# Attention scores as three 64-row passes per head instead of two stacked 128-row products

## The chip, the cores and the metric

The kernel runs on one core of a Trainium2 chip. The metric is the device time of one execution in microseconds (us). A core has TensorE (in the profile PE, its weight loads PEld), VectorE (DVE), ScalarE (ACT), GpSimd (POOL) and SyncE (SP), which here issues all DMA transfers. Matrix products read two operands from on-chip memory (a stationary one, which is loaded as weights, and a moving one, which is streamed past it) and write into a PSUM bank of 512 float32 columns on 128 partitions.

## The reference

The reference is an encoder trunk of two layers on 512 tokens with a model width of 1024. Each layer projects its input once and feeds three token mixers: neighbourhood attention (8 heads of 64), differential attention (4 heads, each with two maps of 64) and latent attention (8 heads of 96). Their outputs are gated, merged and projected, and a SwiGLU FFN follows. What the change touches are the scores of the first two mixers:

```python
# neighbourhood: each query of a 8 x 64 grid sees 8 x 16 keys of it
sc = jnp.einsum('bnqhd,banchd->bhnqac', qb, kb, preferred_element_type=jnp.float32) * scale
...
# differential: two maps per head, each a dense softmax attention over all 512 keys
a1 = blocked_attention(q1, k1, v, scale)
a2 = blocked_attention(q2, k2, v, scale)
o = a1 - lam.astype(a1.dtype) * a2
```

In both, the sum of a score runs over 64 numbers, and `scale` is 1/8.

## The kernel before

All products are made in `float32r`, a float32 format of reduced precision. To come near float32, every operand is split into a high part and a low part (`split`: ScalarE copies the source into the rounded high part, VectorE subtracts that from the source), and a product is a sum of partial products. Projections use three of them, hi x hi, lo x hi and hi x lo (`mm3`, L156 to L158), with 128 rows of the array, since their sums run over multiples of 128.

A score sums over 64 numbers only, which is half of the array's rows. The kernel before fills the other half by stacking. `stacks_q` (L299) makes one tile per head with the high part of q on the head's own 64 rows and the low part on the other 64. `stacks_k` (L311) makes two tiles per head: the high part of k on both halves, and the low part on both halves, the second of which is a copy by DMA (`copy`, L297). Two matmuls of 128 rows then give all four partial products: (q hi, q lo) x (k hi, k hi) and (q hi, q lo) x (k lo, k lo).

The scores stand in two places:

- `na_pair` works on two heads, whose projections share one 128-row tile, and on four blocks `b` of 128 queries with 256 keys each. A block takes one PSUM bank of the kind `sc`, with the two heads side by side. Each head gets two matmuls of 256 columns (L378, L379). VectorE then adds the bias table and finds the maximum (L383), and ScalarE makes the exponentials (L386).
- `df_head` works on one head and four tiles `t` of 128 queries with all 512 keys. Each of the two maps `j` takes one `sc` bank and gets two matmuls of 512 columns (L476, L477). VectorE finds the maximum (L478), and ScalarE makes the exponentials (L479).

There are two `sc` banks, which are used in turn. Around the scores stand the transposes of the weights of attention (L395, L486), their products with the values (L405, L491, L492) and projections of other parts of the layer: `fill` names by a table (`PLAN`) which gate projections (G) and merges (M) are written behind which head. Tiles for q, k, values and activations come from a ring of 38 slots (`R`), so that a slot's next use waits for its last reader.

The order in which each engine gets its instructions is not the order of the code. The tile framework schedules the program with a simulated timeline and places each instruction where it would be ready by that timeline; it can pull matmuls that are written next to each other apart. Each engine then works through its own list in order, and waits are semaphores between the lists.

Of the kernel before, what the change touches and what calls it, by code (L numbers as in the profile page):

```python
# [12 lines left out]
OP = mybir.AluOpType  # L13
# [63 lines left out]
def f32(ap):  # L77
    return ap.bitcast(F32)
# [3 lines left out]
def trunk(ctx, tc, x, ln_in, w_in, feat, bias, lamv, w_mla, w_mlr, w_mlv, w_branch, w_out,  # L82
# [213 lines left out]
    def copy(dst, src):  # L296
        nc.sync.dma_start(f32(dst), f32(src))  # L297

    def stacks_q(p, scale):  # L299

        res = []
        for h in range(2):
            own, oth = (slice(0, 64), slice(64, 128))[::1 if h == 0 else -1]
            t = R.get()
            A.activation(t[own], p[own], AF.Copy, scale=scale)
            V.scalar_tensor_tensor(t[oth], p[own], scale, f32(t[own]), op0=OP.mult, op1=OP.subtract)
            res.append(t)
        return res

    def stacks_k(p):  # L310

        res = []
        for h in range(2):
            own, oth = (slice(0, 64), slice(64, 128))[::1 if h == 0 else -1]
            th, tl = R.get(), R.get()
            A.activation(th[own], p[own], AF.Copy)
            A.activation(th[oth], p[own], AF.Copy)
            V.tensor_sub(tl[own], p[own], f32(th[own]))
            copy(tl[oth], tl[own])
            res.append((th, tl))  # L320
        return res

    def ptsplit(p):
        pp = dp.tile([128, 1024], F32R, tag="PP", name="PP", bufs=2)
# [30 lines left out]
    def na_pair(l, p, vals):  # L355
        src = lambda a, b: [w_in[l, a:b, C_NQ + p * 128:C_NQ + (p + 1) * 128],
                            w_in[l, a:b, C_NK + p * 128:C_NK + (p + 1) * 128]]
        ch = wload_ks(src, 256, (4, 4))
        pq, pk = bank("acc"), bank("acc")
        gemm_w(pq, ch, slice(0, 128), XT, slice(0, S), KD)  # L360
        qs = stacks_q(pq, 0.125)
        gemm_w(pk, ch, slice(128, 256), XT, slice(0, S), KD)
        ks = stacks_k(pk)
        bt = []
        for h in range(2):
            b = H.get()
            nc.sync.dma_start(b[:, :768], bias[l, :, 2 * p + h, :])
            bt.append(b)
        o = (R.get(), R.get())
        o32 = dp.tile([128, 512], F32, tag="o32", name="o32", bufs=1)  # L370
        al, sh = vals
        for b in range(4):
            k0 = (0, 8, 24, 32)[b]
            pat = (0, 1, 1, 2)[b]
            sc = bank("sc").rearrange("p (h k) -> p h k", h=2)
            for h in range(2):
                q = qs[h][:, b * 128:(b + 1) * 128]
                T.matmul(sc[:, h], q, ks[h][0][:, k0 * 8:k0 * 8 + 256], start=True, stop=False)  # L378
                T.matmul(sc[:, h], q, ks[h][1][:, k0 * 8:k0 * 8 + 256], start=False, stop=True)  # L379
            pr = ptile().rearrange("p (h k) -> p h k", h=2)  # L380
            nm, ls = stat(2), stat(2)
            for h in range(2):
                V.tensor_tensor_reduce(out=pr[:, h], in0=sc[:, h], in1=bt[h][:, pat * 256:(pat + 1) * 256],  # L383
                                       op0=OP.add, op1=OP.min, scale=-1.0, scalar=3.0e38,
                                       accum_out=nm[:, h:h + 1])
                A.activation(pr[:, h], pr[:, h], AF.Exp, bias=nm[:, h:h + 1], scale=-1.0,  # L386
                             accum_out=ls[:, h:h + 1])
            rl = stat(2)
            V.reciprocal(rl, ls)
            for h in range(2):  # L390
                V.tensor_scalar(pr[:, h], pr[:, h], rl[:, h:h + 1], None, op0=OP.mult)
            pt = bank("tr").rearrange("p (a h q) -> p a h q", a=2, h=2)
            for a in range(2):
                for h in range(2):
                    T.transpose(pt[:, a, h], pr[:, h, a * 128:(a + 1) * 128], ident)  # L395
            pp = dp.tile([128, 1024], F32R, tag="PP", name="PP", bufs=2)
            split(pp[:, 0:512], pp[:, 512:1024], pt.rearrange("p a h q -> p (a h q)"))
            pp = pp.rearrange("p (s a h q) -> p s a h q", s=2, a=2, h=2)
            po = bank("pv").rearrange("p (h s q) -> p h s q", h=2, s=2)
            for h in range(2):  # L400
                for a in range(2):
                    c0 = k0 + 16 * a
                    v = (al if c0 % 16 == 0 else sh)[c0 // 16][p // 2]
                    v = v[:, (2 * p + h) % 4 * 128:((2 * p + h) % 4 + 1) * 128]
                    T.matmul(po[:, h], v, pp[:, :, a, h], start=a == 0, stop=a == 1)  # L405
            for h in range(2):
                own, oth = (slice(0, 64), slice(64, 128))[::1 if h == 0 else -1]
                oc = o32[own, tsl(b)]
                A.activation(oc, po[oth, h, 0], AF.Copy)
                V.tensor_add(oc, po[own, h, 0], oc)  # L410
                V.tensor_add(oc, po[own, h, 1], oc)
        split(*o, o32)
        R.put(*qs, *ks[0], *ks[1])
        H.put(*bt)
        return o

# [29 lines left out]
    def df_proj(l, h):  # L446
        src = lambda a, b: [w_in[l, a:b, C_DQ + h * 128:C_DQ + (h + 1) * 128],
                            w_in[l, a:b, C_DK + h * 128:C_DK + (h + 1) * 128]]
        ch = wload_ks(src, 256, (4, 4))
        stg = H.get()  # L450
        sv = stg.rearrange("p (t c) -> p t c", t=NT)
        for t in range(NT):
            p = bank("acc")[:, :256]
            gemm_x(p, ch, slice(0, 256), XT, tsl(t), KD)
            A.activation(sv[:, t], p, AF.Copy)
        rope(stg.rearrange("p (t g d) -> p t g d", t=NT, g=4)[:, :, :, 0:16], cosd, sind, 4, 8)
        pq, pk = bank("tr"), bank("tr")
        for t in range(NT):
            T.transpose(pq[:, tsl(t)], sv[:, t, 0:128], ident)
        qs = stacks_q(pq, 0.125)  # L460
        for t in range(NT):
            T.transpose(pk[:, tsl(t)], sv[:, t, 128:256], ident)
        ks = stacks_k(pk)
        H.put(stg)
        return qs, ks

    def df_head(h, qk, vals, nlam, sg):
        qs, ks = qk
        ost = dp.tile([128, 512], F32, tag="o32", name="ost", bufs=1)
        ov = ost.rearrange("p (t d) -> p t d", t=NT)  # L470
        for t in range(NT):
            pr = [ptile(), ptile()]
            nm, ls = stat(2), stat(2)
            for j in range(2):
                sc = bank("sc")
                T.matmul(sc, qs[j][:, tsl(t)], ks[j][0], start=True, stop=False)  # L476
                T.matmul(sc, qs[j][:, tsl(t)], ks[j][1], start=False, stop=True)  # L477
                V.reduce_max(nm[:, j:j + 1], sc, axis=AX.X, negate=True)  # L478
                A.activation(pr[j], sc, AF.Exp, bias=nm[:, j:j + 1], accum_out=ls[:, j:j + 1])  # L479
            rl, cf = stat(2), stat()  # L480
            V.reciprocal(rl, ls)
            V.scalar_tensor_tensor(cf, ls[:, 0:1], rl[:, 1:2], nlam, op0=OP.mult, op1=OP.mult)
            V.scalar_tensor_tensor(pr[0], pr[1], cf, pr[0], op0=OP.mult, op1=OP.add)
            pt = bank("tr")
            for k in range(NT):
                T.transpose(pt[:, tsl(k)], pr[0][:, tsl(k)], ident)  # L486
            ch_, cl_ = ptsplit(pt)
            po = bank("pv")
            for k in range(NT):
                v = vals[k][:, (h % 2) * 256:(h % 2) * 256 + 256]  # L490
                T.matmul(po[:, 0:256], ch_[:, tsl(k)], v, start=k == 0, stop=False)  # L491
                T.matmul(po[:, 0:128], cl_[:, tsl(k)], v[:, 0:128], start=False, stop=k == NT - 1)  # L492
            tmp = sp.tile([128, 128], F32, tag="otmp", name="otmp", bufs=2)
            A.activation(tmp, po[:, 128:256], AF.Copy, scale=rl[:, 0:1])
            V.scalar_tensor_tensor(ov[:, t], po[:, 0:128], rl[:, 0:1], tmp, op0=OP.mult, op1=OP.add)
            ss = stat()
            A.activation(tmp, ov[:, t], AF.Square, scale=128 ** -0.5, accum_out=ss)
            rpow(ss, ss, RMS_EPS)
            V.tensor_scalar(ov[:, t], ov[:, t], ss, None, op0=OP.mult)
        R.put(*qs, *ks[0], *ks[1])  # L500
        pt = bank("tr")
        for t in range(NT):
            T.transpose(pt[:, tsl(t)], ov[:, t], ident)
        o = (R.get(), R.get())
        split(*o, pt, scale=sg)
        return o
# [583 lines left out]
```

## Time and profile before

| | |
|---|---|
| Median of three runs | 1861.91 us (1861.42 to 1862.11) |
| Profiled execution | 1861.61 us, of which the profile's span is 1859.6 us |
| TensorE matmuls | 11200, all with 128 rows |
| TensorE busy | 1814.6 us, 98% of the span |
| VectorE, ScalarE, GpSimd busy | 1331.0, 905.3, 88.2 us |
| Score matmuls, neighbourhood | 128 of 128x256 (L378, L379), 31.2 us busy |
| Score matmuls, differential | 128 of 128x512 (L476, L477), 51.3 us busy |

A row of the groups names the line, the engine, the operation, the tiles written and read, the shape, the count, then the busy time, the mean time of one in ns, the idle time of the engine ahead of it and what ended that idle time. Matmuls are pipelined and their ends are modelled, so the mean time of one is more than the distance from one start to the next; a timeline (start in us, length in us) shows the distances. A wait row names who waited for whom, the total in us, how often, and the longest.

### The profile page before, as it was taken

How to read it: one execution, taken by the hardware profiler on the slowest of the kernel's cores; microseconds unless marked ns; L12 is line 12 of the kernel's file. 1: busy time of each engine (PE TensorE's matmuls, PEld its weight loads, DVE VectorE, ACT ScalarE, POOL GpSimd, SP SyncE). 2: the span in 40 equal slices, each digit the busy share in tenths (PEclk: the TensorE clock that was granted, in tenths of full speed). 3: DMA queues.
4: the chain of work that ended last, by engine and by line, in shares of the span. 5: the costliest groups of instructions: out<-in, count | busy, mean ns of one | idle time of the engine just before them, and what ended most of it. 6: DMA issues, size and time to landing. Idle time of an engine off the chain costs nothing.

```text
span 1859.6 us, 28547 instructions
## 1 busy us (share of the span) xinstructions
PE 1814.6 (98%) x11200; PEld 1617.4 (87%) x11200; DVE 1331.0 (72%) x2228; ACT 905.3 (49%) x1620; POOL 88.2 (5%) x165
## 2 busy tenths in 40 slices
PE   6999999999999899999999999999999999999997
PEld 5988899988878899999789888999888789999996
DVE  6478887665568977777756888866655698677766
ACT  3467776555433433434326677755554244343431
POOL 4100000000001000000001000000000000000001
PEclk9999999999999999999999999999999999999999
DMA  7453332223251233333445432322233512333332
GB/s 250 119 166 88 88 101 74 79 81 85 90 193 58 69 104 101 102 103 102 148 124 156 124 97 87 90 65 86 74 97 109 174 57 90 105 95 110 92 101 79
DMA packets 167765, 195.86 MB, mean 105 GB/s; under 512 B 8528, under 2 KB 132688, under 8 KB 167632
## 3 DMA queue, kind: packets, MB, share of 16 engines
q1 hardware_dynamic: 167632, 194.05, 34.5%
q8 instruction: 88, 1.44, 0.3%
q14 instruction: 45, 0.37, 0.1%
HBM read 177.24 MB, written 9.44 MB: 100 GB/s over the span
## 4 chain that ended last, share of the span: by engine, by line
PE 89%; DVE 4%; DMA 3%; ACT 2%; issue 1%; POOL 1%; POOLq 0%; SPq 0%; DVEq 0%; ACTq 0%
PE acc L156 18%; PE acc L157 18%; PE acc L158 18%; PE sc L778 11%; PE pv L778 8%; PE tr L648 2%; DVE wlo L139 1%; PE pv L491 1%; DMA raw<-in_w_ffn_in_dram 1%; ACT whi L138 1%; PE pv L656 1%; PE pv L655 1%; PE sc L477 1%; PE sc L632 1%; PE sc L631 1%
## 5 line engine op out<-in xcount | busy, mean ns | idle before, releaser
L139 DVE TENSOR_TENSOR wlo<-raw,whi 128x1024 fp32r<-128x1024 f32 (+4 forms) x242 | 288.0, 1191 | 137.0 <-ACT whi L138 132.2
L138 ACT ACTIVATE whi<-raw 128x1024 fp32r<-128x1024 f32 (+4 forms) x242 | 250.0, 1034 | 267.4 <-DMA raw<-in_w_ffn_out_dram 50.9
L138 ACT ACTIVATE whi<-f 128x1024 fp32r<-128x1024 f32 x100 | 104.9, 1057 | 222.4 <-PE acc L158 127.3
L156 PE MATMUL acc<-xth,whi 128*128 128x512 f32 x512 | 203.9, 398 | 0.1
L158 PE MATMUL acc<-xth,wlo 128*128 128x512 f32 x512 | 202.8, 396 | 0.0
L157 PE MATMUL acc<-xtl,whi 128*128 128x512 f32 x512 | 202.6, 396 | 0.0
L156 PE MATMUL acc<-whi,r 128*128 128x512 f32 (+1 forms) x504 | 194.7, 392 | 4.6 <-DVE f L711 3.9
L157 PE MATMUL acc<-wlo,r 128*128 128x512 f32 (+1 forms) x504 | 197.3, 391 | 1.1 <-DVE wlo L139 1.1
L158 PE MATMUL acc<-whi,r 128*128 128x512 f32 (+1 forms) x504 | 197.0, 391 | 0.0
L778 PE MATMUL pv<-r,whi 128*128 128x256 f32 x960 | 175.8, 282 | 9.9 <-DVE P L844 4.8
L156 PE MATMUL acc<-whi,xth 128*128 128x256 f32 (+2 forms) x544 | 161.6, 299 | 2.1 <-ACT whi L138 2.1
L157 PE MATMUL acc<-wlo,xth 128*128 128x256 f32 (+2 forms) x544 | 162.1, 299 | 1.3 <-DVE wlo L139 1.3
L158 PE MATMUL acc<-whi,xtl 128*128 128x256 f32 (+2 forms) x544 | 162.1, 299 | 0.0
L778 PEld LDWEIGHTS pv<-r,whi 128*128 128x128 f32 x960 | 148.2, 189 | 13.4 <-DVE P L844 5.2
L139 DVE TENSOR_TENSOR wlo<-f,whi 128x1024 fp32r<-128x1024 f32 x100 | 121.6, 1221 | 26.0 <-ACT whi L138 25.8
L778 PE MATMUL pv<-r,wlo 128*128 128x256 f32 x480 | 134.7, 281 | 0.0
L778 PE MATMUL sc<-xth,whi 128*128 128x256 f32 x480 | 133.9, 280 | 0.7 <-ACT P L833 0.7
L778 PE MATMUL sc<-xtl,whi 128*128 128x256 f32 x480 | 133.7, 279 | 0.0
L778 PE MATMUL sc<-xth,wlo 128*128 128x256 f32 x480 | 133.3, 279 | 0.0
L156 PEld LDWEIGHTS acc<-whi,r 128*128 128x128 f32 x504 | 94.3, 188 | 26.9 <-DVE f L711 4.7
L157 PEld LDWEIGHTS acc<-wlo,r 128*128 128x128 f32 x504 | 95.0, 188 | 22.1 <-DVE wlo L139 1.8
L158 PEld LDWEIGHTS acc<-whi,r 128*128 128x128 f32 x504 | 94.9, 188 | 21.0
(235 smaller groups left out, 4285.3 us busy)
## 6 DMA issues: line engine op xcount, KB each, us to landing
raw<-in_w_in_dram SPq DMA_DIRECT2D x64, 512.0 KB, 3.8
f<-in_w_ffn_in_dram SPq DMA_DIRECT2D x60, 512.0 KB, 3.7
raw<-in_w_ffn_out_dram SPq DMA_DIRECT2D x44, 512.0 KB, 3.8
raw<-in_w_in_dram SPq DMA_DIRECT2D x64, 256.0 KB, 3.3
raw<-in_w_ffn_in_dram SPq DMA_DIRECT2D x28, 512.0 KB, 3.6
raw<-in_w_branch_dram SPq DMA_DIRECT2D x24, 512.0 KB, 3.5
raw<-in_w_out_dram SPq DMA_DIRECT2D x16, 512.0 KB, 3.8
r<-r SPq DMA_DIRECT2D x56, 128.0 KB, 2.9
```

Of the source, the lines that this page charges most:

```text
L138: A.activation(hi[:, :n], raw[:, :n], AF.Copy)
L139: V.tensor_sub(lo[:, :n], raw[:, :n], f32(hi[:, :n]))
L156: T.matmul(o, lh[0], rh[0], start=first, stop=False)
L157: T.matmul(o, lh[0], rh[1], start=False, stop=False)
L158: T.matmul(o, lh[1], rh[0], start=False, stop=last)
L477: T.matmul(sc, qs[j][:, tsl(t)], ks[j][1], start=False, stop=True)
L491: T.matmul(po[:, 0:256], ch_[:, tsl(k)], v, start=k == 0, stop=False)
L631: T.matmul(sc, q[0][:, tsl(t)], k[0], start=True, stop=False)
L632: T.matmul(sc, q[0][:, tsl(t)], k[1], start=False, stop=False)
L648: T.transpose(pt[:, tsl(i)], prs[i % 2][:, tsl(kp + i // 2)], ident)
L655: T.matmul(oc, v, ph[:, c], start=kt == 0, stop=False)
L778: T.matmul(o[:, c], w[a][:, j, f], x[e], start=fresh and mi == 0 and j == 0 and n == 0, stop=j == 3 and n == 2, skip_group_check=True)
```

## The change

The stacks go. `halves` takes the projection of two heads (or two maps), which lies on the two halves of 128 rows, and splits all of it at once into a high and a low tile with `split`. `scores` then makes three passes, hi x hi, lo x hi and hi x lo, and in each pass one matmul for each half, which reads rows 0 to 63 or 64 to 127 of the tiles alone. The fourth partial product, lo x lo, is not made any more. The two halves write into different PSUM banks: in `na_pair` a bank now holds one head of two blocks (both banks are taken at every second block), and in `df_head` both banks are taken at once for a tile.

```diff
-    def stacks_q(p, scale):
-        res = []
-        for h in range(2):
-            own, oth = (slice(0, 64), slice(64, 128))[::1 if h == 0 else -1]
-            t = R.get()
-            A.activation(t[own], p[own], AF.Copy, scale=scale)
-            V.scalar_tensor_tensor(t[oth], p[own], scale, f32(t[own]), op0=OP.mult, op1=OP.subtract)
-            res.append(t)
-        return res
-
-    def stacks_k(p):
-        res = []
-        for h in range(2):
-            own, oth = (slice(0, 64), slice(64, 128))[::1 if h == 0 else -1]
-            th, tl = R.get(), R.get()
-            A.activation(th[own], p[own], AF.Copy)
-            A.activation(th[oth], p[own], AF.Copy)
-            V.tensor_sub(tl[own], p[own], f32(th[own]))
-            copy(tl[oth], tl[own])
-            res.append((th, tl))
-        return res
+    def halves(p, scale=None):
+        t = (R.get(), R.get())
+        split(*t, p, scale=scale)
+        return t
+
+    def scores(o, q, k, qc, kc):
+        for n, (a, b) in enumerate(((0, 0), (1, 0), (0, 1))):
+            for h in range(2):
+                r = slice(h * 64, h * 64 + 64)
+                T.matmul(o[h], q[a][r, qc], k[b][r, kc], start=n == 0, stop=n == 2)
...
         for b in range(4):
...
-            sc = bank("sc").rearrange("p (h k) -> p h k", h=2)
-            for h in range(2):
-                q = qs[h][:, b * 128:(b + 1) * 128]
-                T.matmul(sc[:, h], q, ks[h][0][:, k0 * 8:k0 * 8 + 256], start=True, stop=False)
-                T.matmul(sc[:, h], q, ks[h][1][:, k0 * 8:k0 * 8 + 256], start=False, stop=True)
+            if b % 2 == 0:
+                scs = [bank("sc") for _ in range(2)]
+            sc = [i[:, b % 2 * 256:b % 2 * 256 + 256] for i in scs]
+            scores(sc, qs, ks, tsl(b), slice(k0 * 8, k0 * 8 + 256))
...
         for t in range(NT):
...
-            for j in range(2):
-                sc = bank("sc")
-                T.matmul(sc, qs[j][:, tsl(t)], ks[j][0], start=True, stop=False)
-                T.matmul(sc, qs[j][:, tsl(t)], ks[j][1], start=False, stop=True)
+            scs = [bank("sc") for _ in range(2)]
+            scores(scs, qs, ks, tsl(t), slice(0, S))
+            for j, sc in enumerate(scs):
                 V.reduce_max(nm[:, j:j + 1], sc, axis=AX.X, negate=True)
...
-        R.put(*qs, *ks[0], *ks[1])
+        R.put(*qs, *ks)
```

In the calls, `stacks_q(pq, 0.125)` and `stacks_k(pk)` become `halves(pq, 0.125)` and `halves(pk)`.

The diff does not show in which order TensorE gets the passes. Two places of its list follow. In the changed kernel L310 is the matmul of `scores`; the number behind `sc` tells the bank's use, and so the half.

First, TensorE in the first neighbourhood pair of the first layer, third block, before: the block's four matmuls of 128 rows into one bank (`sc_914`), two per head, and the first of the next block.

```order
L378 MATMUL sc_914<-r28_102,r26_100 128x256
L379 MATMUL sc_914<-r29_103,r26_100 128x256
L378 MATMUL sc_914<-r30_104,r27_101 128x256
L379 MATMUL sc_914<-r31_105,r27_101 128x256
L378 MATMUL sc_946<-r28_102,r26_100 128x256
```

The same place of the change:

```order
L158 MATMUL acc_1050<-whi_1046,r19_93 128x256
L310 MATMUL sc_910<-r28_102,r26_100 128x256
L310 MATMUL sc_910<-r28_102,r27_101 128x256
L310 MATMUL sc_910<-r29_103,r26_100 128x256
L310 MATMUL sc_911<-r28_102,r26_100 128x256
L310 MATMUL sc_911<-r28_102,r27_101 128x256
L310 MATMUL sc_911<-r29_103,r26_100 128x256
L383 MATMUL tr_891<-cons_120,P_883 128x128 x4
```

The six passes stand together, but half 0 (`sc_910`) comes with all three and then half 1 (`sc_911`); the code has them in turn.

Second, TensorE in the first differential head of the first layer, third tile of queries, before: the two matmuls of one map between projections.

```order
L156 MATMUL acc_3572<-whi_3535,xth_72 128x256
L476 MATMUL sc_3351<-r16_90,r14_88 128x512
L477 MATMUL sc_3351<-r17_91,r14_88 128x512
L157 MATMUL acc_3572<-wlo_3536,xth_72 128x256
L158 MATMUL acc_3572<-whi_3535,xtl_73 128x256
```

The same place of the change:

```order
L158 MATMUL acc_3546<-whi_3535,xtl_73 128x256
L310 MATMUL sc_3347<-r16_90,r14_88 128x512
L310 MATMUL sc_3347<-r16_90,r15_89 128x512
L310 MATMUL sc_3347<-r17_91,r14_88 128x512
L478 MATMUL pv_3288<-r18_92,PP_3285 128x256
L156 MATMUL acc_3546<-whi_3535,xth_72 128x256
L310 MATMUL sc_3348<-r16_90,r14_88 128x512
L479 MATMUL pv_3288<-r18_92,PP_3285 128x128
L478 MATMUL pv_3288<-r19_93,PP_3285 128x256
```

The three passes of map 0 (`sc_3347`) stand alone, with matmuls of 128 rows (products with the values, projections) ahead of and behind them, and those of map 1 (`sc_3348`) follow apart from them. Over the whole program TensorE's list has 11328 matmuls, 384 of them with 64 rows, and these stand in 96 unbroken runs.

More of the change, by code (lines that the diff above doesn't have):

```diff
@@ L360, in na_pair @@
         gemm_w(pq, ch, slice(0, 128), XT, slice(0, S), KD)
-        qs = stacks_q(pq, 0.125)
+        qs = halves(pq, 0.125)
         gemm_w(pk, ch, slice(128, 256), XT, slice(0, S), KD)
-        ks = stacks_k(pk)
+        ks = halves(pk)
         bt = []
@@ L382, in na_pair @@
             for h in range(2):
-                V.tensor_tensor_reduce(out=pr[:, h], in0=sc[:, h], in1=bt[h][:, pat * 256:(pat + 1) * 256],
+                V.tensor_tensor_reduce(out=pr[:, h], in0=sc[h], in1=bt[h][:, pat * 256:(pat + 1) * 256],
                                        op0=OP.add, op1=OP.min, scale=-1.0, scalar=3.0e38,
@@ L459, in df_proj @@
             T.transpose(pq[:, tsl(t)], sv[:, t, 0:128], ident)
-        qs = stacks_q(pq, 0.125)
+        qs = halves(pq, 0.125)
         for t in range(NT):
             T.transpose(pk[:, tsl(t)], sv[:, t, 128:256], ident)
-        ks = stacks_k(pk)
+        ks = halves(pk)
         H.put(stg)
@@ L499, in df_head @@
             V.tensor_scalar(ov[:, t], ov[:, t], ss, None, op0=OP.mult)
-        R.put(*qs, *ks[0], *ks[1])
+        R.put(*qs, *ks)
         pt = bank("tr")
```

## The prediction, made before the changed kernel had run

> **What bounds the kernel now.** I read the page first: span, busy shares, slices, then the chain that ended last.
>
> ```profile
> span 1859.6 us, 28547 instructions
> PE 1814.6 (98%) x11200; PEld 1617.4 (87%) x11200; DVE 1331.0 (72%) x2228; ACT 905.3 (49%) x1620; POOL 88.2 (5%) x165
> PE   6999999999999899999999999999999999999997
> PEclk9999999999999999999999999999999999999999
> PE 89%; DVE 4%; DMA 3%; ACT 2%; issue 1%; POOL 1%; POOLq 0%; SPq 0%; DVEq 0%; ACTq 0%
> ```
>
> TensorE is busy in nearly every slice at full granted clock, and 89% of the chain is its own. The span is a queue of matmuls, so what the change does to the number and spacing of matmuls sets the time; work saved elsewhere counts only where TensorE waits for it. The waits of TensorE and of its weight loads, longest first:
>
> ```profile
> PE tr L263 <- DVE f L253: 11.3, 1, 11.3
> PE pv L778 <- DVE P L844: 4.8, 2, 2.4
> PE acc L156 <- DVE f L711: 3.9, 2, 2.2
> ...
> PE sc L379 <- DMA r<-r: 0.2, 1, 0.2
> ```
> ```profile
> PEld sc L379 <- DMA r<-r: 0.6, 2, 0.5
> PEld sc L477 <- DMA r<-r: 0.3, 1, 0.3
> ```
>
> The long ones lie at layer norm and in the FFN, which the change does not touch. At the scores 0.9 us is all that is waited for, on the copy that builds the key stack. The two attention stretches show the same by windows (us, PE busy, PEld, DVE, ACT, POOL, clock, DMA share, GB/s):
>
> ```profile
> 60.00:180.00 120.00, 119.79 (x671) 104.86 (x670) 92.26 (x262) 79.87 (x187) 8.81 (x16) 1.00 0.45 130
> 300.00:420.00 120.00, 120.00 (x767) 107.89 (x766) 78.87 (x135) 66.19 (x134) 7.57 (x16) 1.00 0.30 83
> ```
>
> **What one matmul costs.** The groups' means are longer than the distance between starts, since matmuls are pipelined:
>
> ```profile
> L379 PE MATMUL sc<-r,r 128*128 128x256 f32 x64 | 16.0, 292 | 0.2 <-DMA r<-r 0.2
> L378 PE MATMUL sc<-r,r 128*128 128x256 f32 x64 | 15.2, 284 | 0.0
> L476 PE MATMUL sc<-r,r 128*128 128x512 f32 x64 | 25.8, 404 | 0.0
> L477 PE MATMUL sc<-r,r 128*128 128x512 f32 x64 | 25.5, 398 | 0.0
> L476 PEld LDWEIGHTS sc<-r,r 128*128 128x128 f32 x64 | 12.1, 189 | 1.3
> ```
>
> So I take distances from the timeline (start, length):
>
> ```profile
> 316.80 0.39 PE L476 MATMUL sc<-r,r 128*128 128x512 f32 x1
> ...
> 322.36 0.39 PE L476 MATMUL sc<-r,r 128*128 128x512 f32 x1
> ```
> ```profile
> 700.01 0.28 PE L778 MATMUL sc<-xth,whi 128*128 128x256 f32 x1
> ...
> 701.66 0.28 PE L778 MATMUL sc<-xth,wlo 128*128 128x256 f32 x1
> ```
>
> From the first to the last of 25 matmuls of 512 columns are 24 steps: 5.56 / 24 = 0.232 us each. From the first to the last of 15 of 256 columns: 1.65 / 14 = 0.118 us. Weight loads lie beside them, but have a floor of their own, which shows where 128-column matmuls stand between 256-column ones (seven loads in a row, first and last, then the matmuls):
>
> ```profile
> 329.94 0.19 PEld L491 LDWEIGHTS pv<-r,PP 128*128 128x128 f32 x1
> ...
> 330.62 0.19 PEld L477 LDWEIGHTS sc<-r,r 128*128 128x128 f32 x1
> ```
> ```profile
> 329.94 0.22 PE L492 MATMUL pv<-r,PP 128*128 128x128 f32 x1
> 330.00 0.33 PE L491 MATMUL pv<-r,PP 128*128 128x256 f32 x1
> 330.16 0.22 PE L492 MATMUL pv<-r,PP 128*128 128x128 f32 x1
> ```
>
> The loads are 0.68 / 6 = 0.113 us apart. A pair of matmuls takes 0.22 to 0.23 us where its columns alone need 0.118 + 0.059 = 0.177: some 0.05 us is lost each time a load could not be hidden.
>
> **The change: the matmuls.** A unit is two heads (or two maps) on 128 queries. It was four matmuls of 128 rows and is six of 64 rows. There are 32 neighbourhood units (4 pairs x 4 blocks x 2 layers, 256 columns) and 32 differential ones (4 heads x 4 tiles x 2 layers, 512 columns): 128 matmuls of each width become 192. If the two halves always ran side by side, a unit would take three steps, not four. Every row of the trace is a full 128-row matmul (128*128), so none shows whether two 64-row ones overlap.
>
> The order of the built program decides more than that. It does not keep the pairs together. The 384 passes stand in 96 unbroken runs between matmuls of 128 rows. Of the 38 neighbourhood runs 12 are three passes of half 0 and then three of half 1, 8 go 0 0 1 1 0 1, 6 alternate fully, and 12 are shorter alternations or a single pass. Of the 58 differential runs 34 are one half's three passes alone, 6 are three and three, 4 alternate fully, and 14 are shorter. I count steps with starts in program order, a half never running two passes at once, and halves overlapping freely. Three and three then take five steps, since only the third and the fourth pass meet; 0 0 1 1 0 1 takes four. The sums are 130 steps of 256 columns (128 before) and 162 of 512 columns (128 before): 62 overlapping pairs and 68 single passes in the first, 30 pairs and 132 single in the second.
>
> - Differential: 34 steps x 0.232 = +7.9 us. A pair's two loads, 2 x 0.113 = 0.226, fit under 0.232.
> - Neighbourhood: a pair of 256 columns is 0.118 by its columns, but 0.226 if its two loads go one after the other. From the columns: 2 x 0.118 = +0.2 us. By the load distance: 62 x 0.226 + 68 x 0.118 - 128 x 0.118 = +6.9 us. I take the second, because 0.113 is the smallest distance between full weight loads in the quoted row of loads; those all go to the same rows, so the first stays as the lower end.
>
> The Trainium skill ("TensorE: Matmul & The Clock Gate", LDWEIGHTS) gives the number of columns over 1.2 GHz as the time of a load, whatever its rows: an estimate of 107 ns for 128 columns, close to the 0.113 us above. Its Part 3 has loads and matmuls of different row groups run together and matmul starts 4 ns apart; by that the lower end would hold and the whole sum come out near 1878 us. No run here shows it yet.
>
> **The change of shape.** Each run is entered and left: 192 changes between 128-row and 64-row matmuls. The trace has none, so I bound one. The lower end is zero, as at the other change of kind that the trace has, plain-f32 transposes between such matmuls:
>
> ```profile
> 86.78 1.03 PE L541 MATMUL tr<-cons,f 128*128 128x128 f32 x8
> 87.56 0.47 PE L156 MATMUL acc<-xth,whi 128*128 128x512 f32 x1
> 87.88 0.39 PE L157 MATMUL acc<-xtl,whi 128*128 128x512 f32 x1
> ```
>
> Eight transposes and one matmul take 1.10 us: 8 x 0.109 + 0.232, with 0.109 about the distance of loads, so nothing is left for the two changes. The upper end is an array that must be empty before the next load starts: the tail of a matmul past its step, 0.398 - 0.232 = 0.166 us (L477's mean), and a load of 0.189, together 0.355 us, or 68 us for 192. I take 0.05 us, the price of a load that could not be hidden in the pairs above, as a change of shape is nearer to that than to an empty array: 192 x 0.05 = +9.6 us.
>
> **The change: what it takes off other engines.**
>
> ```profile
> L305 ACT ACTIVATE r<-acc 64x512 fp32r<-64x512 f32 x16 | 9.5, 592 | 8.9 <-PE acc L158 5.8 <-DVE r L306 2.8
> L317 ACT ACTIVATE r<-acc 64x512 fp32r<-64x512 f32 x16 | 9.5, 594 | 0.2
> L306 DVE SCALAR_TENSOR_TENSOR r<-acc,r 64x512 fp32r<-64x512 f32 x16 | 11.0, 689 | 3.4 <-ACT r L305 3.1
> L221 ACT ACTIVATE PP<-tr 128x512 fp32r<-128x512 f32 x128 | 74.6, 597 | 31.4 <-PE tr L486 14.7 <-PE tr L648 8.5 <-PE tr L395 3.7
> r<-r SPq DMA_DIRECT2D x56, 128.0 KB, 2.9
> ```
>
> A 64-row split costs what a 128-row one does (592 against 597 ns). In each of 16 stack pairs ScalarE had six of these and has two, VectorE had four and has two, and two key copies go: 64 x 0.59 = 38 us of ScalarE, 32 x 0.69 = 22 us of VectorE, and 32 of the 56 copies of 2.9 us on SP's queue. All of it lies beside a busy TensorE. Of it only the 0.9 us at the scores come back: -0.9.
>
> **What is now late.** A score bank holds one head of two blocks, not two heads of one block, so block 2 waits until blocks 0 and 1 have both been read. Behind the waiting pass stand the projection matmuls of the next work. Reading a block is two VectorE operations:
>
> ```profile
> L383 DVE CUSTOM_DVE_ANT_0 P<-sc,f 128x256 f32<-128x256 f32 x64 | 23.8, 418 | 2.6 <-PE sc L379 2.0
> L479 ACT ACTIVATE P<-sc,ring 128x512 f32<-128x512 f32 x64 | 44.0, 688 | 43.5 <-DVE ring L478 42.9
> ```
>
> In the order some twenty other matmuls, of 0.118 to 0.232 us each, stand between two blocks, so I take nothing; without that cover it is 2 x 0.418 x 8 = 6.7 us over 8 pairs. For a differential map the bank is still freed by its own exponential (0.688 us), as before.
>
> **Sum** against this execution's 1861.6 us (span 1859.6 and 2.0 around it; the median of the runs is 1861.9): +7.9 + 6.9 + 9.6 - 0.9 = +23.5, so 1885 us.
>
> **Rivals.**
>
> *The halves do not overlap at all*, that is, the change does not do what it says. For it: no row shows an overlap. Then there are 64 more steps of each width, 64 x (0.118 + 0.232) = +22.4, and with the same 9.6 - 0.9 it ends at 1893 us.
>
> *Each change of shape empties the array.* For it: the trace has one shape alone, so nothing in it shows that two shapes can be in the array at once; against it: the transposes' free change, though that keeps the shape. The price is the tail alone, 192 x 0.166 = +31.9 in place of 9.6: 1907 us. The Trainium skill's "TensorEngine Tiling (Array Packing)", Key Properties, states it as a rule: "Changing tiling mode (not just tile) drains the TensorE". No run here shows it so far.
>
> *Not slower: within a run each half has a queue of its own*, so that a run takes as many steps as its longer half, in whatever order its passes stand, and a change of shape is free. Place: the 26 three-and-three or mixed runs. Then 98 steps of 256 and 150 of 512 columns: -3.5 + 5.1 - 0.9 = +0.7, 1862 us. Against it: in the trace starts keep program order. It decides only if loads of both halves overlap too. The 34 lone triples keep even this from being faster; a gain would need stalls elsewhere to vanish.
>
> **How the numbers follow.** The likeliest, 0.45: 1885, its own range 1877 to 1893 (the lower neighbourhood term, or 0.01 to 0.09 us a change). No overlap 0.2; emptying 0.2; own queues 0.1; 0.05 for others, such as overlap with neither price (+8.1 - 0.9, 1869) or the full 0.355 a change (1861.6 + 14.8 - 0.9 + 68, 1943). The range 1867 to 1910 leaves out own queues, the end of emptying and the worst of the rest. A measurement of this kernel tells 0.2%, 3.7 us, from no change. Faster 0.04 (stalls that vanish beyond the 0.9), same 0.08 (own queues), slower 0.88.
>
> **What would show it.** In the profile after: 11328 matmuls; starts of two alternating 64-row passes almost together (overlap), or 0.118 and 0.232 apart (none); between the two loads of a 256-column pair 0.11 us; at the first 64-row pass and at the first 128-row one after a run a start later than its step by about 0.05 (my term), 0.16 (emptying) or nothing. ScalarE's busy time falls by some 38 us, VectorE's by 22, and neither moves the span. The prediction is wrong if passes of the two halves overlap though they do not stand beside each other, or if new waits of TensorE on VectorE at the score banks exceed some 5 us.

## The result, and the profile after

The changed kernel takes 1891.9 us (median of four runs, 1890.2 to 1893.6) against 1862.0: 1.0161 times as long, with an interval of 1.0143 to 1.0178. The prediction was 1885. The page of the changed kernel:

```profile
span 1888.9 us, 28562 instructions
PE 1849.5 (98%) x11328; PEld 1612.6 (85%) x11328; DVE 1312.5 (69%) x2196; ACT 871.1 (46%) x1556; POOL 87.0 (5%) x165
PEclk9999999999999999999999999999999999999999
```

TensorE is the bound as before. ScalarE gave up 34 us and VectorE 18.5 us of work, and the span grew by 29.3 us. The groups of the score passes, and the weight loads' waits:

```profile
L310 PE MATMUL sc<-r,r 64*128 64x512 f32 x192 | 50.2, 432 | 0.0
L310 PE MATMUL sc<-r,r 64*128 64x256 f32 x192 | 21.7, 317 | 0.0
L310 PEld LDWEIGHTS sc<-r,r 64*128 64x128 f32 x384 | 38.3, 184 | 25.4 <-issue 14.4 <-DVE o L399 1.5 <-DVE PP L222 1.4
```
```profile
PEld sc L310 <- issue: 14.4, 46, 0.4
PEld acc L158 <- issue: 6.1, 18, 0.4
PEld acc L157 <- issue: 4.9, 14, 0.4
```

New is a wait of the weight loads, 0.4 us at most each time, at the passes and at the matmuls behind them; "issue" means that nothing the profile shows held them. The timeline of one run of six passes shows what happens. It is the second tile of the first differential head, whose list has three passes of map 0 and then three of map 1 (start, length; TensorE, then its weight loads):

```profile
326.08 0.39 PE L157 MATMUL acc<-r,whi 128*128 128x512 f32 x1
326.31 0.40 PE L158 MATMUL acc<-r,wlo 128*128 128x512 f32 x1
326.63 0.97 PE L310 MATMUL sc<-r,r 64*128 64x512 f32 x6
327.53 0.66 PE L473 MATMUL tr<-cons,P 128*128 128x128 f32 x4
```
```profile
326.08 0.19 PEld L158 LDWEIGHTS acc<-r,wlo 128*128 128x128 f32 x1
326.63 0.54 PEld L310 LDWEIGHTS sc<-r,r 64*128 64x128 f32 x6 [0.36 <-issue]
327.53 0.20 PEld L473 LDWEIGHTS tr<-cons,P 128*128 128x128 f32 x2 [0.36 <-issue]
```

Six passes last 0.90 us from the first start to the next matmul's (326.63 to 327.53). A lone triple of the same width lasts as long:

```profile
376.21 0.28 PE L156 MATMUL acc<-whi,xth 128*128 128x256 f32 x1
376.42 0.96 PE L310 MATMUL sc<-r,r 64*128 64x512 f32 x3
377.31 0.38 PE L157 MATMUL acc<-wlo,xth 128*128 128x256 f32 x1
377.53 0.28 PE L158 MATMUL acc<-whi,xtl 128*128 128x256 f32 x1
```

That is 0.89 us for three. So the two halves overlap fully, even where the list has three of one and then three of the other: the starts inside such a run come in pairs 10 ns apart (3 to 4 ns where the list has the halves in turn).

The other thing to see is the price of entering and leaving. Three steps of 0.232 are 0.70 us, not 0.90. The matmul ahead of the run is followed after 0.32 us (326.31 to 326.63) where its step is 0.232, and the 256-column matmul behind the triple by 0.22 (377.31 to 377.53) where its step is 0.118. The weight rows show where it goes: the first load of the new shape does not start one step ahead, as loads do otherwise, but together with its own matmul, 0.32 us after the start of the last matmul of the old shape. Over all runs (the steps of the run and of the matmul on either side, less their own 0.232, 0.118, 0.109 or 0.059 us, less the steps of the longer half) a run costs 0.39 us: about 0.09 before the first pass and 0.10 in its first step, and the same again on the way out. That is 0.19 us a change of shape. The 0.09 us on the way in is the same, within 0.01 us on average, whether matmuls of 128, 256 or 512 columns stand ahead. What the first load waits for the trace does not name.

I split the whole span in the same way. Every distance between two starts of TensorE, less the step of the first, is lost time; matmuls other than scores are 1752.8 us of steps in all kernels here, and 20 to 21 us lie ahead of the first and behind the last. The fast FFN products are those that the FFN makes from sums and differences of blocks (`product`, L778 before and L765 in the change); what is lost between two of them has a column of its own. In us:

| Kernel | Median | Span | Scores with their changes of shape | Lost in the fast FFN products | Lost elsewhere |
|---|---|---|---|---|---|
| before | 1862.0 | 1859.6 | 46.5 | 14.2 | 25.4 |
| change | 1891.9 | 1888.9 | 83.5 | 4.2 | 27.8 |
| both halves on rows 0 to 63 | 1918.5 | 1912.6 | 104.1 | 5.3 | 29.9 |
| all passes on 128 rows | 1879.1 | 1879.1 | 67.1 | 7.6 | 30.9 |
| change with spare slots | 1902.4 | 1899.9 | 83.9 | 11.3 | 31.4 |
| change with tiles' halves ready together | 1877.7 | 1875.7 | 68.4 | 4.5 | 29.0 |
| before, low key part by VectorE | 1858.1 | 1856.7 | 47.3 | 5.2 | 31.3 |
| before, high key part by DMA | 1858.0 | 1856.4 | 47.3 | 7.4 | 28.1 |
| before, high key part by VectorE | 1866.1 | 1864.9 | 48.5 | 15.6 | 27.8 |

The scores cost 37.0 us more, 10.0 us were gained in the FFN, which the change does not touch, and 2.4 us were lost elsewhere: together the 29.3 us of the span, within 0.1. The last column moves by up to 6 us from kernel to kernel, and why was not pursued; so a few us of a median stay unexplained.

Each experiment's ratio is to the kernel before in the same session, where its median was 1860.5 us (for the token and the three edits of `stacks_k`) or 1861.1 us (for the others). One of the five executions with the token took 3007.5 us at a granted clock of 0.56, and its ratio leaves that one out.

### The profile page after: what moved, and what is told of

Same layout as the page of the kernel before. It is cut to its first block, busy times and chain, and to the rows that moved or that the text cites. A ratio compares the mean times of both kernels' runs of the same rounds, so it can differ in the third digit from the quotient of the medians.

```text
span 1888.9 us, 28562 instructions
## 1 busy us (share of the span) xinstructions
PE 1849.5 (98%) x11328; PEld 1612.6 (85%) x11328; DVE 1312.5 (69%) x2196; ACT 871.1 (46%) x1556; POOL 87.0 (5%) x165
## 4 chain that ended last, share of the span: by engine, by line
PE 87%; DVE 6%; DMA 3%; ACT 1%; issue 1%; POOLq 0%; DVEq 0%; SPq 0%; POOL 0%; ACTq 0%
PE acc L156 18%; PE acc L157 18%; PE acc L158 18%; PE sc L765 10%; PE pv L765 7%; PE sc L310 3%; DVE wlo L139 2%; PE tr L635 2%; PE pv L478 1%; DMA raw<-in_w_ffn_in_dram 1%; DMA f<-in_w_ffn_in_dram 1%; PE tr L473 1%; DVE r L222 1%; PE pv L643 1%; PE pv L642 1%
## 5 line engine op out<-in xcount | busy, mean ns | idle before, releaser
L765 PE MATMUL pv<-r,whi 128*128 128x256 f32 x960 | 173.2, 280 | 4.2 <-DVE P L831 3.1
L765 PEld LDWEIGHTS pv<-r,whi 128*128 128x128 f32 x960 | 147.1, 188 | 6.9 <-DVE P L831 3.5
L139 DVE TENSOR_TENSOR wlo<-f,whi 128x1024 fp32r<-128x1024 f32 x100 | 121.6, 1221 | 25.7 <-ACT whi L138 25.4
L765 PE MATMUL sc<-xth,wlo 128*128 128x256 f32 x480 | 133.4, 279 | 0.7 <-DVE wlo L139 0.6
L765 PE MATMUL pv<-r,wlo 128*128 128x256 f32 x480 | 133.8, 279 | 0.0
L765 PE MATMUL sc<-xth,whi 128*128 128x256 f32 x480 | 133.7, 279 | 0.0
L765 PE MATMUL sc<-xtl,whi 128*128 128x256 f32 x480 | 133.6, 279 | 0.0
L156 PEld LDWEIGHTS acc<-whi,r 128*128 128x128 f32 x504 | 93.9, 188 | 26.1 <-DVE f L698 4.5
L158 PEld LDWEIGHTS acc<-xth,wlo 128*128 128x128 f32 x512 | 96.3, 188 | 22.3 <-issue 2.7
L156 PEld LDWEIGHTS acc<-xth,whi 128*128 128x128 f32 x512 | 96.3, 188 | 20.9 <-issue 0.7
```

Source lines behind the costliest of these rows:

```text
L139: V.tensor_sub(lo[:, :n], raw[:, :n], f32(hi[:, :n]))
L156: T.matmul(o, lh[0], rh[0], start=first, stop=False)
L158: T.matmul(o, lh[1], rh[0], start=False, stop=last)
L765: T.matmul(o[:, c], w[a][:, j, f], x[e], start=fresh and mi == 0 and j == 0 and n == 0, stop=j == 3 and n == 2, skip_group_check=True)
```

## Experiments

**Is the overlap real, and is it full?** In the first experiment the passes of both halves use the same 64 rows, in the same list order. The second head's scores are then computed from the first head's rows.

```diff
-                r = slice(h * 64, h * 64 + 64)
+                r = slice(0, 64)
```

> Both halves' passes read rows 0 to 63 (the second head's or map's scores are therefore those of the first; the work is wrong in that part, its amount the same). TensorE's list is the changed kernel's, with 384 passes in 96 runs. Theory A (in the changed kernel each half has a queue of its own and the two overlap fully, 98 steps of 256 and 150 of 512 columns): without overlap there are 192 of each, 94 x 0.118 + 42 x 0.232 = +20.8 us on the changed kernel's 1891.9, so about 1913. Rival B (overlap only where the list has the halves in turn, 130 and 162 steps): +14.3, about 1906. Rival C (no overlap; the starts that lie 3 to 10 ns apart in the trace are a matter of recording): no difference, about 1892.

It took 1918.5 us, 1.030 times the kernel before (1.0281 to 1.0319). The run shown above, in this kernel:

```profile
333.56 1.65 PE L310 MATMUL sc<-r,r 64*128 64x512 f32 x6
335.14 0.66 PE L473 MATMUL tr<-cons,P 128*128 128x128 f32 x4
```

Six passes now last 1.58 us instead of 0.90, three steps of 0.23 more. In the profiled executions the scores took 20.6 us more than in the change, where full overlap asked for 20.8, and overlap only where the list has the halves in turn for 14.3; 3 us more were lost outside the scores (the table's last columns), and the rest of the median's 26.6 is the scatter between executions.

**Is it the shape?** In the second experiment each pass reads all 128 rows, and so sums over both heads. Number and order of the matmuls are the change's.

```diff
-                r = slice(h * 64, h * 64 + 64)
+                r = slice(0, 128)
```

> Each pass reads all 128 rows, so that the sums run over both heads or maps (the scores are wrong, the number and order of matmuls is the changed kernel's). There is no change of shape and no overlap. Theory A (a change of shape costs 0.195 us, 192 of them 37.4): +20.8 for the overlap lost and -37.4 for the changes gone, -16.6 on 1891.9, so about 1875, with scores that take 64 x 0.118 + 64 x 0.232 = 22 us more than in the kernel before. Rival (the price lies in the number of matmuls or in the runs' places, not in the shape): about 1913.

It took 1879.1 us, 1.0091 times the kernel before (1.0074 to 1.0107), though it overlaps nothing: 64 more steps of each width and still 12.8 us less than the change. Two places of its timeline, a single pass and a triple with the matmuls behind them:

```profile
330.89 0.39 PE L310 MATMUL sc<-r,r 128*128 128x512 f32 x1
331.12 0.22 PE L479 MATMUL pv<-r,PP 128*128 128x128 f32 x1
...
335.11 0.86 PE L310 MATMUL sc<-r,r 128*128 128x512 f32 x3
335.81 0.28 PE L156 MATMUL acc<-whi,xth 128*128 128x256 f32 x1
```

A pass is followed after 0.23 us and three after 0.70: no extra for coming or going. The scores took 16.4 us less than in the change; 16.6 less were expected from 192 changes at 0.195 us and the overlap given up. Both the price and what it hangs on are settled by this pair.

**Keeping a unit's passes together, first try.** The six passes were wrapped in a section that the scheduler does not take apart.

```diff
+        with tc.tile_critical():
             for n, (a, b) in enumerate(((0, 0), (1, 0), (0, 1))):
```

> The six passes of a unit are kept together in the scheduler as one section, halves in turn: 62 runs instead of 96, no lone triples. Theory A: 62 x 0.38 + 96 x 0.118 + 96 x 0.232 = 57 us of scores against 84 in the changed kernel, -27 on 1891.9, so 1865, plus what the unit now waits for both banks (0 to 10 us), so 1865 to 1875. Rival (a price per 64-row pass, not per change): only the 56 steps that lone halves cost go, -13, so 1879 or more.

It took 1963.4 us, 1.0545 times the kernel before (1.0527 to 1.0564), and so missed every expectation. Its trace says why it does not test the price:

```profile
PE sc L311 <- issue: 16.6, 28, 2.8
...
PE sc L311 <- DMA raw<-in_w_branch_dram: 6.4, 2, 3.4
PE sc L311 <- DMA raw<-in_w_in_dram: 5.7, 3, 3.2
PE sc L311 <- DVE P L380: 5.6, 2, 2.8
```
```profile
PEld sc L311 <- issue: 79.3, 64, 3.7
```

TensorE now waits at the first pass (L311 here) for transfers of other weights and for VectorE work that the scores do not use. By the row of the weight loads, 79.3 us are idle ahead of the 64 units, 1.2 us a unit, with nothing shown that holds them. There are 62 runs, as planned, but by the split above the scores cost 136.9 us, where 57 were expected. The section costs more than the changes of shape that it saves.

**Second try, by data.** A unit falls apart because the bank of map 0 comes free one exponential ahead of that of map 1. So VectorE makes one column of the next tile's q depend on the second exponential (it adds 0 times its sum), in the differential heads alone.

```diff
+    def token(q, c, done):
+        V.scalar_tensor_tensor(q[:, c:c + 1], done, 0.0, f32(q[:, c:c + 1]), op0=OP.mult, op1=OP.add)
...
+            if t < NT - 1:
+                token(qs[0], t * 128 + 128, ls[:, 1:2])
```

> The changed kernel, and in the differential heads a VectorE operation of one column that adds 0 times the second map's sum of exponentials to one column of the next tile's q, so that both halves of the next tile become ready at the same time. The differential runs go from 58 with 150 steps to 48 with 102 (no half alone but for single passes); the neighbourhood runs and the order in the first fast FFN group are the changed kernel's. Theory A (both halves overlap fully, 0.38 us a run): -10 x 0.38 - 48 x 0.232 = -15 on 1891.9, so 1877, plus up to 3 us of waits for the later of the two exponentials. Rival (a price per 64-row pass): only the 48 steps go, -11, 1881 or more, with runs that cost less than 0.38 us.

It took 1877.7 us, 1.0099 times the kernel before (1.0083 to 1.0114), where 1877 was expected. The scores fell by 15.1 us (15.0 expected), and no new wait of TensorE at the passes shows. The second to fourth tile of the first differential head in its timeline, with no lone triple among them:

```profile
326.74 0.96 PE L310 MATMUL sc<-r,r 64*128 64x512 f32 x6
...
333.35 0.96 PE L310 MATMUL sc<-r,r 64*128 64x512 f32 x5
...
334.83 0.50 PE L310 MATMUL sc<-r,r 64*128 64x512 f32 x1
...
340.12 0.97 PE L310 MATMUL sc<-r,r 64*128 64x512 f32 x6
```

So 13 to 14 us of the change's 29.9 were the halves pulled apart in these heads (the medians differ by 14.2, the distances to the kernel before in the same session by 12.7, the spans by 13.2). The rest stays: with 98 steps of 256 and 102 of 512 columns taken off, the 86 runs that are left cost 33 us. The kernel is still 17 us slower than the kernel before.

**Where the 10 us in the FFN come from.** The idle time of TensorE ahead of the fast FFN products fell. Their largest group, before and in the change:

```profile
L778 PE MATMUL pv<-r,whi 128*128 128x256 f32 x960 | 175.8, 282 | 9.9 <-DVE P L844 4.8 <-DVE r L222 2.6 <-DVE P L848 2.3
```
```profile
L765 PE MATMUL pv<-r,whi 128*128 128x256 f32 x960 | 173.2, 280 | 4.2 <-DVE P L831 3.1 <-DVE P L835 1.1
```

Two causes were possible: less work for ScalarE and VectorE, or the order of the lists there, which the scheduler had also changed. Four kernels tell them apart; their TensorE lists around the first fast group are word for word either that of before or that of the change (one departs from it further on, the low key part by VectorE). In the change, two slots more per pair, which nobody uses, bring back the order of before:

```diff
+        spare = (R.get(), R.get())
...
-        R.put(*qs, *ks)
+        R.put(*qs, *ks, *spare)
```

> The changed kernel, but each pair takes two more slots of the ring that nobody uses, six as before the change. The scores stay as they are (96 runs). TensorE's list in the first fast FFN group is that of the kernel before, word for word, while the changed kernel has another there. Theory D (the 7.5 us that the FFN's stalls lost come from that order): they return, about 1899. Rival (they come from less work on ScalarE and VectorE): 1892 as the changed kernel.

It took 1902.4 us, where 1899 was expected. 11.3 us were lost there, 7.1 more than in the change, and 3.6 more in the table's last column:

```profile
L767 PE MATMUL pv<-r,whi 128*128 128x256 f32 x960 | 173.8, 280 | 11.1 <-DVE P L833 4.8 <-DVE P L837 3.4 <-DVE r L222 2.6
```

In the kernel before, three edits of `stacks_k` left the scores' matmuls alone:

```diff
 # the low key part by VectorE
-            copy(tl[oth], tl[own])
+            V.tensor_sub(tl[oth], p[own], f32(th[own]))
 # the high key part by DMA
-            A.activation(th[oth], p[own], AF.Copy)
+            copy(th[oth], th[own])
 # the high key part by VectorE
-            A.activation(th[oth], p[own], AF.Copy)
+            V.tensor_copy(th[oth], p[own])
```

> The kernel before, but VectorE makes the low key part on both halves itself, in place of the 32 copies by DMA (32 more operations of 0.69 us, 22 us of VectorE). The scores stay matmuls of 128 rows. TensorE's list begins the first fast FFN group as the changed kernel's does. Theory D (that order is worth 7.5 us, whatever made it): about 1854, or 1853 with the 0.9 us that the scores waited for the copy; faster than both kernels. Rival (the FFN's stalls went because ScalarE and VectorE had less to do): 1862 or more.

> The kernel before, but the second high key part is copied by DMA, not by ScalarE (32 operations of 0.59 us less there, 32 transfers more). TensorE's list in the first fast FFN group is the changed kernel's, word for word. Theory D: about 1854 to 1856 (more waits for the copies at the scores). Rival (work on the other engines): ScalarE's 19 us less change nothing that TensorE waits for, 1862.

> The kernel before, but VectorE and not ScalarE makes the second high key part. TensorE's list in the first fast FFN group is that of the kernel before, word for word. Theory D: no gain there, about 1862. Rival (less ScalarE work ahead of the FFN): as the others, 1854.

The first two have the new order and took 1858.1 and 1858.0 us, 0.9988 (0.9978 to 0.9998) and 0.9987 (0.9975 to 0.9999) times the kernel before. The third has the old order and took 1866.1, 1.0037 times (1.0023 to 1.0050). The group of the first and of the third:

```profile
L778 PE MATMUL pv<-r,whi 128*128 128x256 f32 x960 | 173.5, 280 | 4.7 <-DVE P L844 2.9 <-DVE P L848 1.7
```
```profile
L778 PE MATMUL pv<-r,whi 128*128 128x256 f32 x960 | 177.0, 284 | 10.4 <-DVE P L844 4.8 <-DVE P L848 2.9 <-DVE r L222 2.6
```

The loss in the fast products goes with the order in all nine kernels of the table: 4.2 to 7.6 us with the new one, 11.3 to 15.6 with the old, whatever the attention does. The kernel with the section, which is not in the table, has both: its first layer begins the group in the new order and lost 2.3 us there, its second has the old order and lost 6.2. VectorE's and ScalarE's lists in the group change together with TensorE's, so the runs show that the schedule there is the cause, not which engine's order. VectorE had more work in the first of these edits, not less, and the gain came all the same. Only a part of it reached the time, 2.4 and 2.5 us against the 1860.5 of the kernel before in that session, where I expected 6 to 8, because the table's last column rose by 5.9 and 2.7 us in these two; what raised it was not pursued. These two are the only kernels here that beat both the kernel before and the change, the former by 0.1%, with intervals that end just short of no difference.

## Why the prediction was right, and where it was not

The time fell into the range, 7 us above the forecast, but by two errors of opposite sign and one thing that was not foreseen: that it came so near is luck. By a sign that the prediction itself named, its mechanism is wrong: "if passes of the two halves overlap though they do not stand beside each other", and they do.

- **Overlap.** My step was "starts in program order", by which three and three take five steps. That is where it failed: each half is worked off for itself, and the steps are 98 and 150, not 130 and 162. The rival "own queues" had this mechanism right. So did the lower end for the neighbourhood term: the two loads of a pair go side by side (a pair of 256 columns takes 0.118 us, loads included), and the 0.113 us between loads holds only for the same rows (with both halves on rows 0 to 63, no two loads of the scores start less than 0.108 us apart). In place of +7.9 + 6.9 stands 98 x 0.118 + 150 x 0.232 less 128 of each, +1.6. The Trainium skill ("TensorE: Matmul & The Clock Gate", Part 3) has the starts of different row groups 4 ns apart, and the trace agrees with 3 to 10 ns; it also has matmuls start strictly in program order, which six passes in three steps contradict for the runs of three and three.
- **Change of shape.** The term was mis-sized: 0.05 us taken, 0.19 measured, so 37.1 us (83.5 less 98 x 0.118 and 150 x 0.232) instead of 9.6. I had taken the smaller loss because it looked like one load not hidden. The rival "emptying" came nearest, with a price (0.166) that was near for another reason: not the modelled tail of a matmul, but 0.09 us until the first load starts and 0.10 us in the first step, about the 0.113 us of a load that nothing hides. The Trainium skill says in "TensorEngine Tiling (Array Packing)", Key Properties, that changing the mode drains TensorE. The trace agrees in that each change costs 0.19 us, and the second experiment shows that nothing is paid as long as the shape stays. That the array is empty at that point the trace does not show: ends of matmuls are modelled, and the last old one in the timeline above is given until 326.71, while the first new load starts at 326.63.
- **The order.** That the scheduler pulls the halves apart, which I read from the list, is right, and it was somewhat less than half of the loss: the token took back 13 to 14 of 29.9 us, though not by the steps I counted.
- **Other engines.** ScalarE fell by 34 us (38 forecast) and VectorE by 18.5 (22 forecast), and neither moved the span. The 0.9 us waited for the stack copy is gone. No wait for a score bank appeared.
- **Not foreseen.** The FFN's 10 us. I had looked only at where the list changed in attention, and put the waits in the FFN aside because the change does not touch it. The edit does not, but the schedule there changed with it.

By the terms: +1.6 for steps, +37.1 for changes, -1.7 for what the scores of before lost beyond their steps (46.5 less 128 of each), -10.0 in the FFN and +2.4 elsewhere make +29.4; I had +14.8, +9.6 and -0.9.

## What to carry to other kernels

Two 64-row matmuls on the two halves of the array run in the time of one (six passes in three steps), but here each run of them costs 0.39 us for coming and going, and a unit saves one step (0.118 or 0.232 us). By these numbers, as an estimate, a run pays from four units of 256 columns or two of 512 on; with 33.6 us of steps if all halves pair up against 46.5 for the stacks, some 33 runs would be break-even, and this program had 96. Before such a change, count the runs in the scheduled order rather than the passes in the code. To keep the halves together, a common dependence served here (1877.7 us), and a section that the scheduler does not take apart did not (1963.4 us).

## What the runs showed that was not expected

Matmuls on the two halves of the rows do not keep the list's order between them: a run of three and three took 0.90 us against 1.58 on one half, which is only possible if the fourth pass of the list starts with the first (the starts lie in pairs 10 ns apart; the trace does not name the half of a pass, but in the list the third and the sixth pass of such a run signal that their bank is done, and in the trace the last two starts do, in all 18 runs of three and three). Weight loads of the two halves run side by side as well, as a neighbourhood run of the change shows:

```profile
98.79 0.42 PEld L310 LDWEIGHTS sc<-r,r 64*128 64x128 f32 x6 [0.36 <-issue]
```

Six loads took 0.42 us from the first start to the last end, where six on the same rows at 0.113 us would take 5 x 0.113 + 0.189 = 0.75. And a reordering that the scheduler made far behind the edit was worth 10 us in the fast products, as much as a third of the whole effect.
